# Forming all activation sums of the down projection in the up stage, with its fourth weight combination on VectorE

## The chip, the cores and the metric

The kernel runs on one core of a Trainium2 chip. The metric is the device time of one execution in microseconds (us). Five engines run their own instruction streams in order and wait for each other by semaphores: TensorE (PE in the profile: matrix products; PEld is its weight load), VectorE (DVE), ScalarE (ACT), GpSimd (POOL) and SyncE (SP), which here only issues DMAs. All times below come from the profile of one execution, or from the three timed runs where that is said.

## The reference

One inference step of a decoder layer in float32, for 512 prompt tokens and 64 sample tokens (8 sequences of 8), 576 columns together:

```python
h = rms_norm(x, norm1)
proj = h @ w_in                       # short conv, dilated attention, pooling
x = x + jnp.concatenate([ya, yb, yc], axis=-1) @ w_out
h2 = rms_norm(x, norm2)
gc, new_ffn = causal_dwconv(h2 @ w_gate, ffn_buf, ffn_conv_w)
x = x + (jax.nn.silu(gc) * (h2 @ w_up)) @ w_down
```

The model width is 2048 and the inner width D_FF is 5504, which is 43 tiles of 128. The outputs are the normed rows and the updated caches and states. This case is about the last line: the activations (43 tiles of 128 x 576) are made in the up stage, written to DRAM, and multiplied by `w_down` in the down stage.

## The kernel before

Every float32 operand is split into a high part in fp32r (a copy on ScalarE) and a low part (what is left, a subtraction on VectorE). A product is then three matmuls: high by high, high by low, low by high.

From the gate projection on, products are made in the Strassen-Winograd form (`strassen_steps`). A pair of 128-column output tiles and the two halves of the inner dimension make a 2x2 matrix of weights, b11, b12, b21, b22; the two 288-column halves of the tokens make the other side. Seven products replace eight. Their weights are, in the order of the steps:

- p1: b11
- s1 (p5 in the code's names of places): b12 - b11
- s2 (u2): b22 - (b12 - b11)
- p2: b21
- s3 (u3): b22 - b12
- s4 (p53): b22
- c21: b21 minus the s2 weights, the fourth combination. Before, GpSimd forms it (L1009) in b21's own tile.

In a step the combination is formed (L990, L998, L1005 on VectorE), the result is split (L933 on ScalarE, L934 on VectorE), the product runs on TensorE (L945), and its sum is taken out of the accumulator. In the down stage that is one addition on VectorE (L1487) for each of six products; a copy on ScalarE (L985) starts the second accumulator. The split weights wh and wl have three buffers each, so a split waits until the product three places earlier is done.

The raw weights lie in tiles of two kinds, wr and wx, with three buffers each, and `raw_tile` alternates between them: b11 and b22 fall into wr, b12 and b21 into wx. SyncE issues the loads in program order, and a load waits on that queue until the last reader of its buffer is done. With three wr buffers, the b22 of a pair takes the buffer of the b11 of the pair before.

The gate and up projections (43 column tiles, 168 matmuls in a pair of tiles) fill the up stage, to about 2060 us. The down stage runs in four chunks of ten activation tiles (NDC = 4, DCHUNK = 5); a chunk is eight pairs of output tiles, a pair has 7 x 15 = 105 matmuls. Three activation tiles are left for a last part.

On the token side each step needs its own combination. For each index i of a chunk (an even tile ae and an odd tile ao) there are four "pieces": "11" (half of ae), "s12", "own" (ao) and "s34". For chunk 0, `first_pieces` reads the sums s12 and s34 from DRAM; `sums` has made them in the up stage for the first five pairs (`if ff < 2 * DCHUNK`). For chunks 1 to 3, `act_pieces` loads ae and ao during the chunk before, forms the sums on VectorE (L1445, L1446, L1452) and splits the pieces (L1442 and L1443, L1455 and L1456, L1453). `PIECE_DUE` says after which step of the chunk each piece is written into the program; what is left over is laid between the first five steps of the next chunk (`going`), where the first two pairs are interleaved. The `late` pair (m == 2) loads its b22 only in its third step.

The order on each engine is made by a scheduler that simulates the program; `high_priority` moves the splits of the first two pairs of each chunk forward.

Of the kernel before, what the change touches and what calls it, by code (L numbers as in the profile page):

```python
# [10 lines left out]
F32 = mybir.dt.float32  # L11
F32R = mybir.dt.float32r
AF = mybir.ActivationFunctionType
# [23 lines left out]
DCHUNK = 5  # L37
NDC = 4
X_TILES = (2, 2, 2, 2, 4, 4)
PIECE_DUE = (4, 8, 12, 16, 19, 22, 25, 28, 31, 34, 37, 40, 46, 47, 47, 48, 49, 50, 51)  # L40
LAST_DUE = (4, 10, 14, 18)
FIRST_PIECES = (2, 3, 2, 2, 2, 2)
AHEAD = (7, 11)
# [40 lines left out]
def decoder_step(ctx: ExitStack, tc, I, O):  # L84
# [883 lines left out]
    def strassen_steps(load, X, evac, split, n, urgent=False, late=False):  # L968


        w = n * P
        strn[0] += 1
        tag = "s" if strn[0] % 2 else "pt"
        c = X.c

        def first():
            return tc.high_priority(offset=200) if urgent else nullcontext()

        a, b = bank("a")[:, :HALF], bank("b")[:, :HALF]
# [12 lines left out]
        product(e, hl, c["s1"], True)  # L992
        evac("p5", e)
        yield
        b22 = load(1, 1) if late else b22
        b21 = load(1, 0)
        with first():
            nc.vector.tensor_sub(b11[:, :w], b22[:, :w], b11[:, :w])  # L998
            hl = split(w, b11[:, :w])
        product(a, hl, c["s2"], False)  # L1000
        evac("u2", a)
        yield
        with first():
            hl = split(w, b21[:, :w])
            nc.vector.tensor_sub(b12[:, :w], b22[:, :w], b12[:, :w])  # L1005
        product(b, hl, c["12"], False)
        evac("p2", b)
        yield
        nc.gpsimd.tensor_sub(b21[:, :w], b21[:, :w], b11[:, :w])  # L1009
        with first():  # L1010
            hl = split(w, b12[:, :w])
        product(a, hl, c["s3"], False)
        evac("u3", a)
        yield
        with first():
            hl = split(w, b22[:, :w])
        product(e, hl, c["s4"], False)
        evac("p53", e)
        yield
        with first():  # L1020
            hl = split(w, b21[:, :w])
        product(a, hl, c["22"], False)
        evac("c21", a)
        yield
# [214 lines left out]
    def state_out(nst, f0, nf):  # L1239
# [4 lines left out]
        for f in range(nf):  # L1244
# [14 lines left out]

    def sums(i, g1, g2):  # L1260
# [21 lines left out]
        now.setdefault(kind, []).append(name)  # L1282
        return slot_of(name)

    def first_pieces(X, n):

        half = [work() for _ in range((n + 1) // 2)]
        for i in range(n):
            j = i % 2 * HALF
            dma(half[i // 2][:, j:j + HALF], act_d[2 * i][:, :HALF])  # L1290

        def load(src):
            t = work()
            dma(t, src)
            return t

        raw = {("s12", i): load(sum_d[i][0]) for i in range(n)}
        yield
        for i in range(n):
            if i % 2 == 0:  # L1300
                t11 = next_slot("11")
            hl = single_of(t11, i % 2)
            src = half[i // 2][:, i % 2 * HALF:(i % 2 + 1) * HALF]
            with_unit(nc.scalar.activation(hl[0], src, AF.Copy))
            nc.vector.tensor_sub(hl[1], src, hl[0].bitcast(F32))
            X.put("11", i, hl)
            yield
        todo = [(c, i) for c in ("s12", "own", "s34") for i in range(n)]
        for c, i in todo:
            if c == "own" and i == 0:  # L1310
                raw.update({("own", k): load(act_d[2 * k + 1]) for k in range(n - 1)})
            if c == "own" and i == n - 1:
                raw.update({("own", n - 1): load(act_d[2 * n - 1])})
                raw.update({("s34", k): load(sum_d[k][1]) for k in range(n)})
            t = next_slot(c)
            src = raw[c, i]
            with_unit(nc.scalar.activation(t[:, 0], src, AF.Copy))
            nc.vector.tensor_sub(t[:, 1], src, t[:, 0].bitcast(F32))
            for name, hl in zip({"s12": ("s2", "s1"), "own": ("12", "22"), "s34": ("s4", "s3")}[c], pair_of(t)):
                X.put(name, i, hl)  # L1320
            yield

    x1 = []
# [16 lines left out]
    for nf in GROUPS:  # L1340
# [8 lines left out]
        if f0 == 0:  # L1349
            begun = {0: gate_pair(ht, 0, 0, urgent=True), 2: gate_pair(ht, 2, 2, urgent=True, late=True)}  # L1350
            advance(begun[0][2], 3)
            advance(begun[2][2], 2)
        for f in range(0, nf, 2):
            ff = f0 + f
            if f + 1 < nf:
# [20 lines left out]
            if ups and nf > 1:  # L1376
                for _ in up_steps(*ups.pop(0)):
                    pass
                go_on(len(later))
# [4 lines left out]


    nextX = Halves(DCHUNK)
    nxt = first_pieces(nextX, DCHUNK)
    steps = up_steps(*ups.pop(0))
    next(steps)
    next(nxt)  # L1390
    free.extend(n_ for k in RELEASE for n_ in rest[k])
    for n_ in FIRST_PIECES:
        next(steps)
        for _ in range(n_):
# [18 lines left out]

    AL = 6

    def act_tile(k):
        t = fp.tile([P, TOK], F32, tag="al", bufs=AL, name=nm("al"))
        dma_paced(t, act_d[k])
        return t

    def act_pieces(X, k0, n):

        al, t11 = [], {}
        order_ = [(c, i) for i in range(n - 2) for c in ("11", "s12", "own", "s34")]
        order_ += [(c, i) for i in (n - 2, n - 1) for c in ("11", "s12")]
        order_ += [(c, i) for c in ("own", "s34") for i in (n - 2, n - 1)]
        names = {(c, i): free.pop(0) for c, i in order_ if c != "11" or i % 2 == 0}
        for (c, _), name in names.items():
            now.setdefault(c, []).append(name)

        def load():
            if len(al) < n:
                i = len(al)
                al.append((act_tile(k0 + 2 * i), act_tile(k0 + 2 * i + 1)))

        def piece(c, i):
            ae, ao = al[i]
            if c == "11":
                if i % 2 == 0:
                    t11[i // 2] = slot_of(names[c, i])  # L1440
                hl = single_of(t11[i // 2], i % 2)
                with_unit(nc.scalar.activation(hl[0], ae[:, :HALF], AF.Copy))  # L1442
                nc.vector.tensor_sub(hl[1], ae[:, :HALF], hl[0].bitcast(F32))  # L1443
                X.put("11", i, hl)
                nc.vector.tensor_add(ae[:, HALF:], ae[:, HALF:], ao[:, HALF:])  # L1445
                nc.vector.tensor_sub(ae[:, :HALF], ae[:, HALF:], ae[:, :HALF])  # L1446
                return
            t = slot_of(names[c, i])
            src = ae if c == "s12" else ao
            if c == "s34":  # L1450
                s2 = ae[:, :HALF].unsqueeze(1).to_broadcast([P, 2, HALF])
                with_unit(nc.vector.tensor_sub(halves(ao), halves(ao), s2))  # L1452
                nc.scalar.activation(t[:, 0], src, AF.Copy)  # L1453
            else:
                with_unit(nc.scalar.activation(t[:, 0], src, AF.Copy))  # L1455
            nc.vector.tensor_sub(t[:, 1], src, t[:, 0].bitcast(F32))  # L1456
            for name, hl in zip({"s12": ("s2", "s1"), "own": ("12", "22"), "s34": ("s4", "s3")}[c], pair_of(t)):
                X.put(name, i, hl)
            if c == "s34":
                load()  # L1460

        for _ in range(AL // 2):
            load()
        yield
        for c, i in order_:
            piece(c, i)
            yield

    def last_pieces(k0, n):

# [23 lines left out]
    for ci in range(NDC):  # L1494
# [2 lines left out]
            chunk_done()  # L1497
        if ci < NDC - 1:
            nextX = Halves(DCHUNK)
            nxt = act_pieces(nextX, f0 + nf, DCHUNK)  # L1500
            due = PIECE_DUE
        else:
            nxt = last_pieces(f0 + nf, NF - f0 - nf)
# [17 lines left out]
            pass  # L1521
        if ci == 0:
            chunk_done()
        for steps in pairs:
            load_x1(min(KD, len(x1) + 2))
            for _ in steps:
# [126 lines left out]
```

## Time and profile before

| | |
|---|---|
| three timed runs, median (lowest, highest) | 2643.67 us (2643.23, 2647.12) |
| the profiled execution, its own time | 2641.39 us |
| its span, first to last instruction | 2639.5 us |
| mean granted TensorE clock | 0.988 |
| busy: PE, DVE, ACT, POOL | 2551.3, 1920.6, 972.1, 622.8 us |

The busy time of PE is no measure of its pace, since matmuls overlap. In a stretch the count of matmuls says more: where nothing is waited for, the stretch from 2480 to 2562 us shows 619 of them in 82 us, 7.55 for each us.

### The profile page before, as it was taken

What the parts mean: (1) busy time and instruction counts of PE and PEld (TensorE: products, weight loads), DVE (VectorE), ACT (ScalarE), POOL (GpSimd) and SP (SyncE); (2) the same over time, 40 slices, a digit from 0 to 9 for tenths busy, and PEclk for the clock granted to TensorE, in tenths of its full rate; (3) what the DMA queues carried; (4) which work ended last, traced back from release to release, by engine and by line L of the source; (5) the groups of instructions that cost most, each with busy time, mean ns of one, the idle gap of its engine ahead of it and who ended that gap; (6) DMA issues with size and microseconds to landing.
All of it is one profiled execution on the core that took longest, in us unless ns stands there. A gap on an engine that the chain in (4) does not pass through costs nothing.

```text
span 2639.5 us, 48741 instructions
## 1 busy us (share of the span) xinstructions
PE 2551.3 (97%) x19855; PEld 2495.6 (95%) x19855; DVE 1920.6 (73%) x2619; ACT 972.1 (37%) x1445; POOL 622.8 (24%) x460
## 2 busy tenths in 40 slices
PE   8999989989999999999999999999999999989997
PEld 7999889989989999999999999999999998989897
DVE  5667766865766544597878787877777888888875
ACT  6121221222121233354444444444444544444445
POOL 0434334434443000022222121212121111101014
PEclk9999989989999999999999999999999999999999
DMA  8547457537655696556555555555555865555534
GB/s 272 140 122 182 134 148 194 164 110 197 167 152 168 179 281 196 162 181 194 172 185 157 177 153 169 161 166 161 169 162 175 286 183 152 148 147 168 160 100 150
DMA packets 608210, 451.47 MB, mean 171 GB/s; under 512 B 22967, under 2 KB 570082, under 8 KB 601586
## 3 DMA queue, kind: packets, MB, share of 16 engines
q1 hardware_dynamic: 591358, 438.72, 56.0%
q10 hardware_dynamic: 16628, 9.64, 1.2%
q8 instruction: 156, 2.56, 0.4%
q14 instruction: 68, 0.56, 0.1%
HBM read 402.75 MB, written 132.81 MB: 203 GB/s over the span
## 4 chain that ended last, share of the span: by engine, by line
PE 83%; DVE 8%; DMA 6%; issue 1%; ACT 1%; SPq 0%; POOL 0%; DVEq 0%; ACTq 0%
PE a L945 27%; PE acc L176 11%; PE acc L178 10%; PE acc L177 10%; PE pt L945 7%; PE s L945 6%; PE b L945 6%; DMA ev<-in_cache_kv_w_dram 2%; DVE wl L934 2%; DMA al<-act 1%; DVE av L594 1%; DVE xs L1456 1%; DMA wr<-in_w_down_dram 1%; DVE wl L153 1%; PE ps L569 1%
## 5 line engine op out<-in xcount | busy, mean ns | idle before, releaser
L945 PE MATMUL a<-xs,wh 128*128 128x288 f32 x4032 | 814.4, 296 | 14.2 <-ACT wh L933 8.4
L945 PEld LDWEIGHTS a<-xs,wh 128*128 128x128 f32 x4032 | 647.7, 189 | 21.0 <-ACT wh L933 10.7
L176 PE MATMUL acc<-xs,wh 128*128 128x288 f32 x2208 | 663.4, 301 | 0.0
L177 PE MATMUL acc<-xs,wh 128*128 128x288 f32 x2208 | 657.1, 298 | 0.4 <-DVE xs L203 0.3
L178 PE MATMUL acc<-xs,wl 128*128 128x288 f32 x2208 | 655.9, 297 | 0.2 <-DVE wl L153 0.2
L945 PE MATMUL a<-xs,wl 128*128 128x288 f32 x2016 | 592.6, 295 | 1.6 <-DVE wl L934 1.6
L933 ACT ACTIVATE wh<-wr 128x1024 fp32r<-128x1024 f32 (+1 forms) x300 | 276.7, 924 | 519.7 <-PE a L945 210.9
L176 PEld LDWEIGHTS acc<-xs,wh 128*128 128x128 f32 x2208 | 417.5, 189 | 8.4 <-issue 7.6
L178 PEld LDWEIGHTS acc<-xs,wl 128*128 128x128 f32 x2208 | 419.5, 190 | 4.4 <-issue 3.9
L177 PEld LDWEIGHTS acc<-xs,wh 128*128 128x128 f32 x2208 | 418.5, 190 | 1.7 <-DVE xs L200 0.6
L945 PEld LDWEIGHTS a<-xs,wl 128*128 128x128 f32 x2016 | 378.5, 188 | 2.9 <-DVE wl L934 2.7
L1009 POOL TENSOR_TENSOR wx<-wx,wr 128x1024 f32<-128x1024 f32 (+1 forms) x75 | 161.7, 2157 | 883.3 <-DVE wl L934 747.7
L152 ACT ACTIVATE wh<-wr 128x1024 fp32r<-128x1024 f32 (+1 forms) x150 | 155.4, 1037 | 581.7 <-PE acc L177 505.3
L934 DVE TENSOR_TENSOR wl<-wr,wh 128x1024 fp32r<-128x1024 f32 (+1 forms) x300 | 316.1, 1055 | 73.1 <-ACT wh L933 70.0
L934 DVE TENSOR_TENSOR wl<-wx,wh 128x1024 fp32r<-128x1024 f32 (+1 forms) x225 | 273.8, 1223 | 84.7 <-ACT wh L933 84.5
L153 DVE TENSOR_TENSOR wl<-wr,wh 128x1024 fp32r<-128x1024 f32 (+1 forms) x150 | 242.7, 1619 | 105.5 <-ACT wh L152 99.1
L933 ACT ACTIVATE wh<-wx 128x1024 fp32r<-128x1024 f32 (+1 forms) x225 | 206.5, 921 | 169.7 <-PE b L945 85.9
L945 PE MATMUL s<-xs,wh 128*128 128x288 f32 x1024 | 208.0, 295 | 0.0
L945 PE MATMUL b<-xs,wh 128*128 128x288 f32 x1008 | 206.7, 296 | 0.3
L945 PE MATMUL pt<-xs,wh 128*128 128x288 f32 x992 | 203.1, 297 | 3.7 <-ACT wh L933 3.7
L499 POOL TENSOR_TENSOR eq<-qb,ek 128x1024 f32<-128x1024 f32 x48 | 123.1, 2565 | 224.7 <-DMA ek<-in_cache_kv_w_dram 104.4
L499 POOL TENSOR_TENSOR prod<-qb,ek 128x1024 f32<-128x1024 f32 x48 | 122.7, 2557 | 189.6 <-PE acc L176 102.6
(321 smaller groups left out, 3662.5 us busy)
## 6 DMA issues: line engine op xcount, KB each, us to landing
out_dram<-in_cache_kv_w_dram SPq DMA_DIRECT2D x320, 204.0 KB
wr<-in_w_in_dram SPq DMA_DIRECT2D x110, 512.0 KB
ek<-in_cache_kv_w_dram SPq DMA_DIRECT2D x52, 512.0 KB
ev<-in_cache_kv_w_dram SPq DMA_DIRECT2D x52, 512.0 KB
wx<-in_w_gate_dram SPq DMA_DIRECT2D x43, 512.0 KB
wr<-in_w_gate_dram SPq DMA_DIRECT2D x43, 512.0 KB
wr<-in_w_up_dram SPq DMA_DIRECT2D x43, 512.0 KB
wx<-in_w_up_dram SPq DMA_DIRECT2D x43, 512.0 KB
```

The costliest lines, as they stand in the source:

```text
L152: nc.scalar.activation(hi[:, :n], dst, AF.Copy)
L153: low.tensor_sub(lo[:, :n], dst, hi[:, :n].bitcast(F32))
L176: mark.append(nc.tensor.matmul(o, wh, xh, start=first, stop=False))
L177: nc.tensor.matmul(o, wh, xl, start=False, stop=False)
L178: nc.tensor.matmul(o, wl, xh, start=False, stop=last)
L499: with_unit(nc.gpsimd.tensor_mul(pv_, c["q"], keys))
L569: nc.tensor.matmul(o[32 * j:32 * j + 32, :P], pm[:, c:c + 32], rhs, start=i < 4, stop=i >= len(terms) - 4, tile_position=(0, 32 * j), skip ...
L594: i_ = nc.vector.scalar_tensor_tensor(av[:, t, :], v[:, t, :], w, av[:, t, :], op0=ALU.mult, op1=ALU.add)
L933: nc.scalar.activation(hi[:, :n], src, AF.Copy)
L934: nc.vector.tensor_sub(lo[:, :n], src, hi[:, :n].bitcast(F32))
L945: mm = nc.tensor.matmul(o, a[:, ws], b, start=first and k == 0 and i == 0, stop=k == n - 1 and i == 2, skip_group_check=True)
L1009: nc.gpsimd.tensor_sub(b21[:, :w], b21[:, :w], b11[:, :w])
```

## The change

All sums of the down stage's activations, for 20 pairs of tiles and not for 5, are now made in the up stage and stored in DRAM (`sum_d` has NDC * DCHUNK entries). One `act_pieces` serves all four chunks: it loads the needed piece itself (half tiles for "11", s12, ao, s34) and only splits it. The pieces come in the order "11", "s12", "own", "s34" for the whole chunk, with six (chunk 0: eight) loads ahead, and at other steps than before. The fourth weight combination is written into b11's tile instead of b21's, one step earlier, and in the down projection (n = 5) it is made by VectorE; in the gate and up projections (n = 8) it stays on GpSimd. The late pair gets a step of its own for the load of its b22. In the up stage the extra `go_on` after each pair is left out.

```diff
-PIECE_DUE = (4, 8, 12, 16, 19, 22, 25, 28, 31, 34, 37, 40, 46, 47, 47, 48, 49, 50, 51)
+PIECE_DUE = (2, 5, 8, 11, 14, 17, 20, 23, 27, 31, 35, 39, 42, 45, 46, 48, 50)
...
-        b22 = load(1, 1) if late else b22
+        if late:
+            b22 = load(1, 1)
+            yield
         b21 = load(1, 0)
...
             nc.vector.tensor_sub(b12[:, :w], b22[:, :w], b12[:, :w])
+            (nc.gpsimd if n == 8 else nc.vector).tensor_sub(b11[:, :w], b21[:, :w], b11[:, :w])
         product(b, hl, c["12"], False)
         evac("p2", b)
         yield
-        nc.gpsimd.tensor_sub(b21[:, :w], b21[:, :w], b11[:, :w])
...
         with first():
-            hl = split(w, b21[:, :w])
+            hl = split(w, b11[:, :w])
         product(a, hl, c["22"], False)
...
-             for i in range(DCHUNK)]
+             for i in range(NDC * DCHUNK)]
...
-        if ff < 2 * DCHUNK:
+        if ff < 2 * NDC * DCHUNK:
             sums(ff // 2, g1, g2)
...
+    def act_pieces(X, c, tile_, dma_, ahead_):
...
+        todo = [(kind, i) for kind in ("11", "s12", "own", "s34") for i in range(n)]
...
+        def load(kind, i):
+            t = raw[kind, i] = tile_()
+            r = n * c + i
+            dma_(t, {"s12": sum_d[r][0], "own": act_d[k0 + 2 * i + 1], "s34": sum_d[r][1]}[kind])
...
+            with_unit(nc.scalar.activation(d0, src, AF.Copy))
+            nc.vector.tensor_sub(d1, src, d0.bitcast(F32))
...
-                nc.vector.tensor_add(ae[:, HALF:], ae[:, HALF:], ao[:, HALF:])
-                nc.vector.tensor_sub(ae[:, :HALF], ae[:, HALF:], ae[:, :HALF])
...
-                with_unit(nc.vector.tensor_sub(halves(ao), halves(ao), s2))
```

The new order on VectorE in the middle of a chunk (chunk 2). wl<-wr, wl<-wx are low parts of weights, L1487 takes a product out, L1456 splits a piece. Before, from the split of b22 of one pair to the s2 combination of the next:

```order
L934 TENSOR_TENSOR wl_26031<-wr_25918,wh_26030 128x640
L1487 TENSOR_TENSOR wk_22956<-b_25913,wk_22956 128x288
L934 TENSOR_TENSOR wl_26051<-wx_25962,wh_26050 128x640
L1487 TENSOR_TENSOR wk_22958<-a_25912,wk_22958 128x288
L934 TENSOR_TENSOR wl_26085<-wr_26078,wh_26084 128x640
L990 TENSOR_TENSOR wr_26078<-wx_26080,wr_26078 128x640
L1487 TENSOR_TENSOR wk_22958<-pt_25940,wk_22958 128x288
L1456 TENSOR_TENSOR xs_26070<-al_25783,xs_26070 128x576
L1005 TENSOR_TENSOR wx_26080<-wr_26082,wx_26080 128x640
L934 TENSOR_TENSOR wl_26107<-wr_26078,wh_26106 128x640
L1487 TENSOR_TENSOR wk_22956<-a_25912,wk_22956 128x288
L998 TENSOR_TENSOR wr_26078<-wr_26082,wr_26078 128x640
```

The same stretch now (L1467 takes a product out, L1341 splits a piece, L1007 and L1000 are the former L1005 and L998):

```order
L934 TENSOR_TENSOR wl_25154<-wr_25034,wh_25153 128x640
L1467 TENSOR_TENSOR wk_23316<-b_25029,wk_23316 128x288
L934 TENSOR_TENSOR wl_25174<-wr_25030,wh_25173 128x640
L1341 TENSOR_TENSOR xs_25148<-al_24554,xs_25148 128x576
L1467 TENSOR_TENSOR wk_23318<-a_25028,wk_23318 128x288
L934 TENSOR_TENSOR wl_25205<-wr_25198,wh_25204 128x640
L990 TENSOR_TENSOR wr_25198<-wx_25200,wr_25198 128x640
L1467 TENSOR_TENSOR wk_23318<-pt_25061,wk_23318 128x288
L1007 TENSOR_TENSOR wx_25200<-wr_25202,wx_25200 128x640
L934 TENSOR_TENSOR wl_25227<-wr_25198,wh_25226 128x640
L1467 TENSOR_TENSOR wk_23316<-a_25028,wk_23316 128x288
L1000 TENSOR_TENSOR wr_25198<-wr_25202,wr_25198 128x640
```

The third row, the split for c21, now reads b11's tile (wr) and no longer b21's (wx); the first reader of the next b22 (L1007) stands six rows behind it.

On SP in the middle of chunk 0 (wr and wx are the weights, the copies between them are cache rows from DRAM to DRAM). Before, the loads of one pair, b11, b12, b21 and, fifth, b22:

```order
L1511 DMA wr_24029<-in_w_down_dram 128x5x128 [waits DMAHW1_49,DVE_49]
L1511 DMA wx_24031<-in_w_down_dram 128x5x128 [waits DMAHW2_49,DVE_49]
L1511 DMA wx_24081<-in_w_down_dram 128x5x128 [waits DMAHW3_49,DVE_49]
L140 DMA out_dram<-in_cache_kv_w_dram 16x3264 [waits DMAHW4_49]
L1511 DMA wr_24033<-in_w_down_dram 128x5x128 [waits DMAHW5_49,Pool_49]
L140 DMA out_dram<-in_cache_kv_w_dram 16x3264 [waits DMAHW6_49]
```

Now, b21 (wx_24052) and b22 (wr_24008) of one pair, then b12 and b11 of the next, then a piece:

```order
L1491 DMA wx_24052<-in_w_down_dram 128x5x128 [waits DMAHW7_49,DVE_49]
L140 DMA out_dram<-in_cache_kv_w_dram 16x3264 [waits DMAHW0_49]
L140 DMA out_dram<-in_cache_kv_w_dram 16x3264 [waits DMAHW1_49]
L140 DMA out_dram<-in_cache_kv_w_dram 16x3264 [waits DMAHW2_49]
L1491 DMA wr_24008<-in_w_down_dram 128x5x128 [waits DMAHW3_49,DVE_49]
L1491 DMA wx_24174<-in_w_down_dram 128x5x128 [waits DMAHW4_49]
L1491 DMA wr_24172<-in_w_down_dram 128x5x128 [waits DMAHW5_49,DVE_49]
L140 DMA al_23977<-s34e_11944 128x576 [waits DMAHW6_49,DVE_49]
```

The load of b22 waited for POOL (the reader of b11 was L1009) and stood one copy behind b21; it now waits for DVE (the reader is the c21 split of the pair before) and stands three copies behind b21.

On VectorE at the start of chunk 1, where pair 0 ends and pair 1 (the late one) goes on. Before:

```order
L934 TENSOR_TENSOR wl_24383<-wr_24217,wh_24382 128x640
L1487 TENSOR_TENSOR wk_22786<-b_24212,wk_22786 128x288
L934 TENSOR_TENSOR wl_24403<-wx_24269,wh_24402 128x640
L998 TENSOR_TENSOR wr_24294<-wr_24437,wr_24294 128x640
L1005 TENSOR_TENSOR wx_24296<-wr_24437,wx_24296 128x640
```

Now:

```order
L934 TENSOR_TENSOR wl_24523<-wr_24351,wh_24522 128x640
L1467 TENSOR_TENSOR wk_22933<-b_24346,wk_22933 128x288
L934 TENSOR_TENSOR wl_24557<-wr_24347,wh_24556 128x640
L1467 TENSOR_TENSOR wk_22935<-a_24345,wk_22935 128x288
L1000 TENSOR_TENSOR wr_24429<-wr_24500,wr_24429 128x640
L1007 TENSOR_TENSOR wx_24431<-wr_24500,wx_24431 128x640
```

In both, pair 1's b22 (wr_24437, wr_24500) is first read two or so rows behind pair 0's c21 split; now that split is also the last reader of the buffer (b11 of pair 0, wr_24347) into which this b22 is loaded.

## Rows read from the trace of the kernel before

**Rows 1.** Windows: length, busy (instructions) of PE, PEld, DVE, ACT, POOL; clock, DMA, GB/s
```profile
1188.00:2046.00 858.00, 858.00 (x6478) 857.77 (x6478) 671.79 (x821) 372.99 (x475) 192.32 (x189) 1.00 0.55 169
2080.00:2106.00 26.00, 22.76 (x153) 20.38 (x152) 23.47 (x37) 12.02 (x20) 2.04 (x1) 1.00 1.06 363
2106.00:2204.00 98.00, 94.96 (x698) 92.61 (x697) 86.39 (x132) 43.79 (x69) 13.86 (x7) 1.00 0.58 169
2204.00:2233.00 29.00, 23.41 (x150) 22.70 (x149) 21.35 (x34) 9.80 (x15) 3.12 (x2) 0.88 0.48 151
2233.00:2328.00 95.00, 92.00 (x678) 89.78 (x677) 83.41 (x127) 43.18 (x68) 11.71 (x6) 1.00 0.53 154
2328.00:2359.00 31.00, 25.21 (x162) 23.92 (x161) 23.68 (x37) 10.01 (x16) 3.12 (x2) 0.89 0.54 162
2359.00:2455.00 96.00, 93.21 (x688) 91.21 (x687) 84.63 (x129) 43.55 (x69) 11.71 (x6) 1.00 0.51 149
2455.00:2480.00 25.00, 20.33 (x143) 18.81 (x142) 20.39 (x31) 9.72 (x15) 1.57 (x1) 1.00 0.60 200
2480.00:2562.00 82.00, 82.00 (x619) 81.80 (x618) 67.36 (x99) 32.31 (x48) 9.44 (x6) 1.00 0.42 123
```

**Rows 2.** Waits of PE from 2204 to 2233 us: total, times, longest
```profile
PE pt L945 <- DVE wl L934: 2.4, 1, 2.4
PE a L945 <- ACT wh L933: 2.1, 1, 2.1
```

**Rows 3.** Groups by line and shape, 2040 to 2580 us: busy us, mean ns
```profile
L934 DVE TENSOR_TENSOR wl<-wr,wh 128x640 fp32r<-128x640 f32 x128 | 105.7, 828 | 20.1 <-ACT wh L933 19.3
...
L934 DVE TENSOR_TENSOR wl<-wx,wh 128x640 fp32r<-128x640 f32 x96 | 84.8, 898 | 6.4 <-ACT wh L933 6.4
...
L1009 POOL TENSOR_TENSOR wx<-wx,wr 128x640 f32<-128x640 f32 x32 | 58.1, 1817 | 441.2 <-DVE wl L934 391.9 <-DMA act<-wk 27.2 <-PE s L945 12.3
...
L1456 DVE TENSOR_TENSOR xs<-al,xs 128x576 fp32r<-128x576 f32 x45 | 49.7, 1108 | 0.0
...
L1452 DVE TENSOR_TENSOR al<-al,al 128x576 f32<-128x576 f32 x15 | 11.2, 749 | 1.7 <-PE s L945 1.7
...
L1445 DVE TENSOR_TENSOR al<-al,al 128x288 f32<-128x288 f32 x15 | 8.2, 544 | 7.9 <-DMA al<-act 7.9
...
L1446 DVE TENSOR_TENSOR al<-al 128x288 f32<-128x288 f32 x15 | 6.5, 446 | 0.0
```

**Rows 4.** Timeline of POOL and DVE near 2180 us: start, duration, instruction
```profile
2180.20 2.03 POOL L1009 TENSOR_TENSOR wx<-wx,wr 128x640 f32<-128x640 f32 x1 [12.01 <-DVE wl L934]
...
2180.72 2.13 DVE L1456 TENSOR_TENSOR xs<-al,xs 128x576 fp32r<-128x576 f32 x1
```

**Rows 5.** Timeline of DVE and PE in the last chunk, 2541 to 2552 us
```profile
2541.91 0.83 DVE L934 TENSOR_TENSOR wl<-wx,wh 128x640 fp32r<-128x640 f32 x1 [0.24 <-ACT wh L933]
...
2545.80 0.81 DVE L1005 TENSOR_TENSOR wx<-wr,wx 128x640 f32<-128x640 f32 x1
...
2549.34 0.82 DVE L934 TENSOR_TENSOR wl<-wr,wh 128x640 fp32r<-128x640 f32 x1 [0.89 <-ACT wh L933]
...
2551.19 0.29 PE L945 MATMUL a<-xs,wl 128*128 128x288 f32 x1
```

**Rows 6.** Timelines of SP and DVE, 2212 to 2227 us: DMA issues, their readers
```profile
2212.77 0.32 SPq L140 DMA_DIRECT2D al<-act  x1
...
2215.72 0.46 DVE L1445 TENSOR_TENSOR al<-al,al 128x288 f32<-128x288 f32 x1 [0.42 <-DMA al<-act]
...
2220.98 0.48 SPq L1511 DMA_DIRECT2D wr<-in_w_down_dram  x1
...
2222.57 0.83 DVE L934 TENSOR_TENSOR wl<-wx,wh 128x640 fp32r<-128x640 f32 x1 [0.24 <-ACT wh L933]
...
2226.17 0.83 DVE L998 TENSOR_TENSOR wr<-wr,wr 128x640 f32<-128x640 f32 x1 [2.77 <-DMA wr<-in_w_down_dram]
```

**Rows 7.** Groups on DVE, 1188 to 1386 us: the last of the three sums
```profile
L1271 DVE TENSOR_TENSOR wk<-wk,wk 128x576 f32<-128x576 f32 x5 | 3.8, 758 | 0.2
```

More of the change, by code (lines that the diff above doesn't have):

```diff
@@ L1283, in next_slot @@
         return slot_of(name)
[L1285 to L1297, printed above, removed]
-        yield
[L1299 to L1320, printed above, removed]
@@ new lines, in act_pieces, with load11, load_to @@
+    def act_pieces(X, c, tile_, dma_, ahead_):
+        n = DCHUNK
+        k0 = 2 * n * c
+        todo = [(kind, i) for kind in ("11", "s12", "own", "s34") for i in range(n)]
+        names = {}
+        loads = []
+        raw = {}
+        def load11(i):
+            t = tile_()
+            for k in range(i, min(i + 2, n)):
+                part = t[:, (k - i) * HALF:(k - i + 1) * HALF]
+                dma_(part, act_d[k0 + 2 * k][:, :HALF])
+                raw["11", k] = part
+        def load(kind, i):
+            t = raw[kind, i] = tile_()
+            r = n * c + i
+            dma_(t, {"s12": sum_d[r][0], "own": act_d[k0 + 2 * i + 1], "s34": sum_d[r][1]}[kind])
+        for kind, i in todo:
+            if kind != "11":
+                loads.append((kind, i))
+            elif i % 2 == 0:
+                loads.append((kind, i))
+        at_ = 0
+        def load_to(m):
+            nonlocal at_
+            while at_ < min(m, len(loads)):
+                kind, i = loads[at_]
+                load11(i) if kind == "11" else load(kind, i)
+                at_ += 1
+        load_to(ahead_)
+        yield
+        for kind, i in todo:
+            if kind != "11" or i % 2 == 0:
+                names[kind, i] = free.pop(0)
+                now.setdefault(kind, []).append(names[kind, i])
+        for j, (kind, i) in enumerate(todo):
+            src = raw[kind, i]
+            if kind == "11":
+                if i % 2 == 0:
+                    t11 = slot_of(names[kind, i])
+                d0, d1 = single_of(t11, i % 2)
+                X.put("11", i, (d0, d1))
+            else:
+                t = slot_of(names[kind, i])
+                d0, d1 = t[:, 0], t[:, 1]
+                for name, hl in zip({"s12": ("s2", "s1"), "own": ("12", "22"), "s34": ("s4", "s3")}[kind], pair_of(t)):
+                    X.put(name, i, hl)
+            with_unit(nc.scalar.activation(d0, src, AF.Copy))
+            nc.vector.tensor_sub(d1, src, d0.bitcast(F32))
+            del raw[kind, i]
+            done_ = loads.index((kind, i - i % 2 if kind == "11" else i)) + (kind != "11" or i % 2 or i + 1 == n)
+            load_to(done_ + ahead_)
@@ L1352, in decoder_step @@
             advance(begun[2][2], 2)
+            advance(begun[0][2], 1)
+            advance(begun[2][2], 1)
         for f in range(0, nf, 2):
@@ L1378, in decoder_step @@
                     pass
-                go_on(len(later))
             if f + 1 < nf:
@@ L1386, in decoder_step @@
     nextX = Halves(DCHUNK)
-    nxt = first_pieces(nextX, DCHUNK)
+    nxt = act_pieces(nextX, 0, work, dma, 8)
     steps = up_steps(*ups.pop(0))
     next(steps)
+    free.extend(n_ for k in RELEASE for n_ in rest[k])
     next(nxt)
-    free.extend(n_ for k in RELEASE for n_ in rest[k])
     for n_ in FIRST_PIECES:
@@ L1414, in decoder_step, with al_tile @@
     AL = 6
+    def al_tile():
+        return fp.tile([P, TOK], F32, tag="al", bufs=AL, name=nm("al"))
     def act_tile(k):
-        t = fp.tile([P, TOK], F32, tag="al", bufs=AL, name=nm("al"))
+        t = al_tile()
         dma_paced(t, act_d[k])
         return t
[L1421 to L1444, printed above, removed]
-                nc.vector.tensor_add(ae[:, HALF:], ae[:, HALF:], ao[:, HALF:])
-                nc.vector.tensor_sub(ae[:, :HALF], ae[:, HALF:], ae[:, :HALF])
[L1447 to L1451, printed above, removed]
-                with_unit(nc.vector.tensor_sub(halves(ao), halves(ao), s2))
[L1453 to L1467, printed above, removed]
     def last_pieces(k0, n):
@@ L1499, in decoder_step @@
             nextX = Halves(DCHUNK)
-            nxt = act_pieces(nextX, f0 + nf, DCHUNK)
+            nxt = act_pieces(nextX, ci + 1, al_tile, dma_paced, AL)
             due = PIECE_DUE
@@ L1523, in decoder_step @@
             chunk_done()
+        next(pairs[0])
+        next(pairs[1])
         for steps in pairs:
```

## Prediction

> **What bounds the kernel now.** I first read the windows [rows 1], because the busy share of PE (97% of the span) hides its pace: matmuls overlap, so I count them. In the stretch from 2480 to 2562 us, 619 matmuls start in 82 us, 7.55 for each us; the up stage from 1188 to 2046 us shows 6478 in 858 us, also 7.55. That is full pace, and a stretch's loss is its length less its matmuls divided by 7.55. The chunk starts lose 26 - 153/7.55 = 5.7 us (chunk 0), 9.1 (chunk 1), 9.5 (chunk 2) and 6.1 (chunk 3), together 30.4. The interiors of chunks 0, 1 and 2 lose 5.5, 5.2 and 4.9, together 15.6; the last chunk's interior loses nothing. So 46.0 us is all that the down stage can give back, and the up stage has nothing to give.
>
> What separates the last interior from the others is VectorE: 86.39/98, 83.41/95 and 84.63/96, all 88% busy, against 67.36/82 = 82% [rows 1]. ScalarE lies at 39 to 45% and DMA between 0.42 and 0.58. The last chunk prepares no pieces for a next one. I read this as VectorE pacing the interiors of chunks 0 to 2.
>
> At a chunk start the waits of PE [rows 2] name the low part of a weight (2.4 us at once) and a high part (2.1 us at once). The second has a transfer behind it: VectorE's combination stood 2.77 us for the late pair's b22 [rows 6]. The granted clock is 0.88 and 0.89 in two of the four starts and 1.00 elsewhere [rows 1], so part of each runs at the lower level, 1.2 GHz and not 2.4, after PE had stood. A share of 0.12 lost over 29 us is 3.5 us, and 0.11 over 31 us is 3.4: 6.9 of the 30.4 us.
>
> **The change part by part.** All sums are against the profiled execution, 2641.39 us by its own time (span 2639.5, 1.9 around it); the median of the three runs is 2.3 us above it, and I take the saving from the median.
>
> *VectorE in the interiors.* The sums of chunks 1 to 3 go: 8.2 + 6.5 + 11.2 = 25.9 us, 8.6 for a chunk [rows 3]. The fourth combination comes: 32 times 0.81 us, the duration of the combination beside it [rows 5], 26 us, 6.5 for a chunk. So far this is an exchange. But GpSimd's 32 instructions (1.817 us each, 58.1 us) go as well, and beside one of them a piece's split on VectorE took 2.13 us [rows 4] against about 0.75 for an operation of the same width, L1452 [rows 3]. The means carry it: 45 splits at 1.108 less 0.749 make 16.2 us, 96 splits from wx at 0.898 less 0.828 make 6.7 us. The pieces' splits lie in three chunks and those from wx in four, so that is 16.2/3 + 6.7/4 = 7.1 us for a chunk. VectorE then has 8.6 + 7.1 - 6.5 = 9.2 us less of some 97 in a chunk, 79% instead of 88%, below the 82% at which nothing is lost. Bounds of the interior's loss by this alone: 0 (last chunk) to 15.6 us (as now).
>
> *Up stage.* Fifteen more pairs of tiles get sums, 0.76 us [rows 7] and two of half the width at 0.45 (L1446, [rows 3]), 1.7 us a pair, 25 us, and two stores each. VectorE there is 671.79/858 = 78% busy, PE at full pace, and in that very window five pairs already have sums. I cost it at nothing. The cover is VectorE's 186 us of idle time; were it gone, the 25 us would show.
>
> *The new wait for b22.* With three wr buffers, b22 of a pair takes b11's of the pair before. Its last reader was GpSimd; it is now the c21 split on VectorE, four products later than b11's own use. In the last chunk [rows 5] that split ends at 2541.91 + 0.83 = 2542.74, and b22's first reader, the combination for s3, starts at 2545.80, 3.1 us after it. It need not start there: the low part for s2 is ready at 2549.34 + 0.82 = 2550.16, and PE's first matmul with it starts at 2551.19, 1.0 us later. A landing up to about 4.0 us after the issue costs PE nothing. Every us beyond costs 1 us in 24 pairs (32 less the two at the head of each chunk). Behind the waiting combination stand the s1 split and the next products' evacuations, which is how it reaches PE; behind the load on SP's queue stand the next pair's b12 and b11 and one piece, which have buffers and time.
>
> Landings, bounded by rows [rows 6]: an activation tile issued at 2212.77 is read at 2215.72 (2.9 us, its reader waiting); a b22 issued at 2220.98, with another load ahead of it, is read at 2226.17 (5.2 us, its reader waiting). In the interiors b22 stands behind three copies of cache rows, which I put between: 3.6 to 4.2 us, at the threshold and nearer to the 2.9 us row, since b21 itself went out long before. I take 5 us for all interiors of chunks 0 to 2 (0.2 us in each of 24 pairs), ends 0 and 24 x 1.2 = 29 us, and 1 us for the last chunk (0 to 6).
>
> [...]
>
> *Chunk starts.* The first gap comes from pieces bunched at steps 46 to 51 and their wait for activation tiles; the pieces are now spread evenly from step 2 on and only split. I take 5.2 us to 2.5 a start. The second gap, the late pair's b22, is now issued only behind pair 0's c21 split, at 2222.57 + 0.83 = 2223.40 instead of 2220.98 [rows 6], 2.4 us later, but with no load just ahead of it; at 2.9 us it lands at 2226.3, as now, at 5.2 us at 2228.6. I keep 2.2 us (0 to 4.7). Half of the low-clock time goes with the first gap. Together 30.4 becomes 22, ends 15 and 36. The start of the up stage has the same dependence once or twice: 2 us (0 to 4).
>
> *Sum.* 46.0 becomes 5 + 1 + 22 + 2 = 30: 16 us saved by the terms, of which I count 14, since the chunk starts are the least certain. 2643.67 - 14 = 2629.5 us. About 5 us (0.2%) is what a measurement of this kernel can tell from no change.
>
> **The rivals.**
> *A: the chunk starts fall too.* If both gaps close, PE does not stand and the clock stays at 1.00 there; the starts fall to 15 or less and the interiors to 2: 28 us, 2615 us. For it: the pieces are spread over the whole chunk. Against: b22 of pair 1 is issued later.
> *B: the wait for b22 takes the gain back.* Landing at 4.6 to 4.9 us costs 0.6 to 0.9 us in 24 pairs, 14 to 22 us: 2638 to 2644 us. For it: the threshold of 4.0 us lies inside the two rows; and the copies ahead of it. Against: DMA is half idle [rows 1].
> *C: slower.* The same mechanism decides from the other end: each b22 lands as when queued behind a load, 5.2 us and a little more for the extra 3.5 instead of 2 tiles loaded for each index. 1.5 us in 24 pairs is 36 us, the starts stay at 30: 2660 to 2665 us. It decides above 4.0 us of landing, and turns to slower at about 4.9.
> *D: an even exchange.* If what stretched VectorE's rows was not GpSimd, 25.9 us out and 26 in leave the interiors at 88%: 2643 us. For it: the longer means of splits could have a cause that stays. Against: 2.13 beside 0.75 us while GpSimd was at work [rows 3, 4].
> The Trainium skill speaks of this ("Perfetto Trace Analysis", section "Optimizing Scalar/DVE Operations"): where VectorE is saturated, work may go from it to GpSimd, though the two share a read port and it might not help. Its first half is against this change, its second for it. By the 2.13 us [rows 4] the second holds here.
>
> **How the numbers follow.** The forecast (2629.5, from 2622 to 2637) 0.52, A 0.15, B 0.17, C 0.11, D 0.05. Faster by over 0.2%, below 2638.4: forecast, A, and a third of B, 0.72. Within 0.2%: D and most of B, 0.17. Slower: C, 0.11. The range from 2614 to 2645 holds the forecast, nearly all of B and D and most of A, and leaves out C.
>
> **What would show it.** Windows of the three interiors at 7.5 matmuls for each us and VectorE near 79% there; no splits of 2 us on VectorE in the down stage; the combination for s3 (now L1007) with an idle time before it that ends by a DMA of under 1 us a pair, and PE without waits behind it; the clock at 1.00 over the chunk starts; the up stage from 1188 us still at 7.55. I am wrong if L1007 or L1000 stand over 1 us for b22 in most pairs (B, C), if the up stage falls behind its pace, or if VectorE stays at 88% (D).

## The result, and the profile after

The changed kernel took 2658.93 us (median of 9 runs, 2652.37 to 2666.45) against 2642.99 us for the kernel before on the same chips: the ratio is 1.0058, 95% interval 1.0043 to 1.0074. It is slower by about 15 us, where 14 us faster was forecast.

I cut both profiled executions at the same products. A chunk's first 210 matmuls (its two interleaved pairs) are its start, the other 630 its interior; the loss is the length less the matmuls divided by 7.55. The windows cut after by these bounds (columns as in [rows 1]) are:

```profile
2087.40:2124.70 37.30, 32.06 (x213) 30.56 (x212) 26.38 (x43) 13.93 (x23) 0.00 (x0) 0.91 0.80 259
2124.70:2219.30 94.60, 88.58 (x632) 84.20 (x632) 75.53 (x119) 40.57 (x64) 0.00 (x0) 1.00 0.63 186
2219.30:2254.20 34.90, 31.08 (x211) 29.53 (x211) 25.64 (x41) 13.23 (x22) 0.00 (x0) 0.95 0.57 178
2254.20:2345.80 91.60, 87.60 (x632) 84.05 (x631) 73.05 (x116) 39.80 (x63) 0.00 (x0) 1.00 0.59 169
2345.80:2381.00 35.20, 31.52 (x213) 29.67 (x212) 25.43 (x40) 13.28 (x22) 0.00 (x0) 0.95 0.58 180
2381.00:2470.90 89.90, 87.74 (x632) 84.00 (x631) 73.50 (x116) 39.77 (x63) 0.00 (x0) 1.00 0.59 170
2470.90:2503.80 32.90, 29.95 (x212) 28.10 (x211) 24.70 (x38) 12.50 (x20) 0.00 (x0) 1.00 0.59 191
2503.80:2592.00 88.20, 85.03 (x628) 83.18 (x627) 65.75 (x103) 33.41 (x51) 1.72 (x2) 1.00 0.37 104
```

At full pace 630 matmuls take 83.4 us. The four interiors (rows two, four, six and eight) take 94.6, 91.6, 89.9 and 88.2. The loss by this cut, in us, each from one profiled execution:

| | up stage | four starts | four interiors | median, us |
|---|---|---|---|---|
| before | 5.8 | 31.3 | 17.7 | 2642.99 |
| changed | 7.8 | 29.1 | 31.5 | 2658.93 |

The two profiled executions differ by 17.6 us of span: 13.8 in the interiors, -2.2 in the starts, 2.0 in the up stage, and 4.2 ahead of the gate projection, where nothing was changed. That last term is scatter: over all kernels of this study the stretch ended between 1113.9 and 1124.2 us, in no order with what was changed. The up stage from 1188 to 2046 us still shows 6479 matmuls in 858 us, its full pace.

What the interiors wait for stands in the groups by line and shape from 2080 to 2590 us (busy us, mean ns, then idle time ahead and its releaser):

```profile
L1341 DVE TENSOR_TENSOR xs<-al,xs 128x576 fp32r<-128x576 f32 x45 | 33.8, 751 | 0.1
...
L1007 DVE TENSOR_TENSOR wx<-wr,wx 128x640 f32<-128x640 f32 x32 | 26.3, 823 | 37.2 <-DMA wr<-in_w_down_dram 37.2
L1000 DVE TENSOR_TENSOR wr<-wr,wr 128x640 f32<-128x640 f32 x32 | 26.1, 817 | 13.9 <-DMA wr<-in_w_down_dram 13.8
L1008 DVE TENSOR_TENSOR wr<-wx,wr 128x640 f32<-128x640 f32 x32 | 26.1, 816 | 0.0
```

L1008 is the new combination: 26.1 us, as worked out. L1341 splits a piece in 0.751 us where L1456 took 1.108 [rows 3]: the stretch beside GpSimd is gone. But L1007, the combination for s3 and the first reader of b22 in most pairs, now stands 37.2 us for its load. In the kernel before, over the same window, the two readers of b22 (L1005 and L998 there) waited for it almost only at the late pairs of the chunk starts (L998):

```profile
L1005 DVE TENSOR_TENSOR wx<-wr,wx 128x640 f32<-128x640 f32 x32 | 26.2, 818 | 0.8 <-DMA wr<-in_w_down_dram 0.7
L998 DVE TENSOR_TENSOR wr<-wr,wr 128x640 f32<-128x640 f32 x32 | 26.2, 818 | 9.8 <-DMA wr<-in_w_down_dram 9.7
```

One wait of L1007, in the timeline of the changed kernel in chunk 0 (start, duration, instruction, idle time ahead in brackets):

```profile
2149.87 1.79 SPq L140 DMA_DIRECT2D out_dram<-in_cache_kv_w_dram  x3
...
2150.44 0.82 DVE L934 TENSOR_TENSOR wl<-wr,wh 128x640 fp32r<-128x640 f32 x1
...
2151.75 0.53 SPq L1491 DMA_DIRECT2D wr<-in_w_down_dram  x1
...
2152.16 0.83 DVE L934 TENSOR_TENSOR wl<-wr,wh 128x640 fp32r<-128x640 f32 x1 [0.18 <-ACT wh L933]
...
2159.37 0.82 DVE L1007 TENSOR_TENSOR wx<-wr,wx 128x640 f32<-128x640 f32 x1 [2.91 <-DMA wr<-in_w_down_dram]
2160.11 0.82 DVE L934 TENSOR_TENSOR wl<-wr,wh 128x640 fp32r<-128x640 f32 x1
...
2160.99 0.40 PE L945 MATMUL pt<-xs,wl 128*128 128x288 f32 x1 [1.30 <-DVE wl L934]
```

Read from the top: three copies are issued, then b22 at 2151.75. L1007 starts at 2159.37, 7.6 us later, as soon as it has landed. Behind L1007 stands the split for s1 (2160.11), and TensorE waits for that split (2160.99), though s1 needs nothing of b22.

The rows also correct the prediction, and the section on the change, on who releases the buffer. b22 is issued behind the split of 2150.44, which is that of the preceding pair's b22 (for s4), and ahead of the end of the c21 split (2152.16 + 0.83 = 2152.99). In the program's placement of tiles a b22 takes the preceding pair's b11 before the change, and in the changed kernel the preceding pair's b22, in every pair: b11's tile now lives up to the c21 split, so b22's own is the first to come free. In the last listing of that section the releasing split is the first row (wl_24523 from wr_24351) and not the third.

Over the 32 pairs, counted from the issue to the last of a load's 16 landing events, b22 lands after 6.03 us (median); in the kernel before it was 4.89.

### The profile page after: what moved, and what is told of

It reads as the page before. It is cut to its first block, busy times and chain, and to the rows that moved or that the text cites. A ratio compares the mean times of both kernels' runs of the same rounds, so it can differ in the third digit from the quotient of the medians.

```text
span 2657.1 us, 48811 instructions
## 1 busy us (share of the span) xinstructions
PE 2564.5 (97%) x19855; PEld 2501.1 (94%) x19855; DVE 1958.9 (74%) x2651; ACT 966.4 (36%) x1445; POOL 598.7 (23%) x428
## 5 line engine op out<-in xcount | busy, mean ns | idle before, releaser
L933 ACT ACTIVATE wh<-wr 128x1024 fp32r<-128x1024 f32 (+1 forms) x375 | 345.9, 923 | 623.8 <-PE a L945 211.5
L934 DVE TENSOR_TENSOR wl<-wr,wh 128x1024 fp32r<-128x1024 f32 (+1 forms) x375 | 394.0, 1051 | 76.7 <-ACT wh L933 74.9
L152 ACT ACTIVATE wh<-wr 128x1024 fp32r<-128x1024 f32 (+1 forms) x150 | 155.4, 1037 | 586.8 <-PE acc L177 528.7
L153 DVE TENSOR_TENSOR wl<-wr,wh 128x1024 fp32r<-128x1024 f32 (+1 forms) x150 | 245.2, 1636 | 103.9 <-ACT wh L152 99.8
L1008 POOL TENSOR_TENSOR wr<-wx,wr 128x1024 f32<-128x1024 f32 x43 | 139.8, 3250 | 648.2 <-DVE wl L934 570.8
L934 DVE TENSOR_TENSOR wl<-wx,wh 128x1024 fp32r<-128x1024 f32 (+1 forms) x150 | 184.3, 1236 | 16.7 <-ACT wh L933 16.0
L945 PEld LDWEIGHTS s<-xs,wh 128*128 128x128 f32 x1024 | 164.0, 188 | 5.9 <-ACT wh L933 4.3
L945 PEld LDWEIGHTS b<-xs,wh 128*128 128x128 f32 x1008 | 163.0, 189 | 5.7 <-ACT wh L933 5.4
```

Source lines behind the costliest of these rows:

```text
L152: nc.scalar.activation(hi[:, :n], dst, AF.Copy)
L153: low.tensor_sub(lo[:, :n], dst, hi[:, :n].bitcast(F32))
L933: nc.scalar.activation(hi[:, :n], src, AF.Copy)
L934: nc.vector.tensor_sub(lo[:, :n], src, hi[:, :n].bitcast(F32))
L945: mm = nc.tensor.matmul(o, a[:, ws], b, start=first and k == 0 and i == 0, stop=k == n - 1 and i == 2, skip_group_check=True)
L1008: (nc.gpsimd if n == 8 else nc.vector).tensor_sub(b11[:, :w], b21[:, :w], b11[:, :w])
```

## The experiments

Each kernel is the changed one with one edit, where nothing else is said. The reference of each ratio is the kernel before on the same chip.

**The tile of the combination.** VectorE forms it still, in b21's tile, one step later.

```diff
-            (nc.gpsimd if n == 8 else nc.vector).tensor_sub(b11[:, :w], b21[:, :w], b11[:, :w])
+            if n == 8:
+                nc.gpsimd.tensor_sub(b11[:, :w], b21[:, :w], b11[:, :w])
...
         evac("p2", b)
         yield
+        if n != 8:
+            with first():
+                nc.vector.tensor_sub(b21[:, :w], b21[:, :w], b11[:, :w])
```

> The changed kernel, but in the down stage VectorE writes the fourth combination into b21's tile, one step later, so that b11's buffer is free after that combination and not after the c21 split. Theory 1 (the wait for b22): b22 is issued two products earlier, its landing of 6.0 us (median of the changed kernel) ends before its reader, the loss of the interiors falls from 31.5 us to 10 or less, and the time to 2630 to 2640 us. Theory 2 (the work itself, 26 us more on VectorE and more bytes loaded): nothing of that is changed, the time stays at 2655 to 2663 us.

Measured: 2618.77 us, ratio 0.9915 (0.9891 to 0.9938). Interiors 4.1 us, starts 18.0. The same 32 instructions on the same engine, written into another tile, make 38 us less (0.9915 against 1.0058). The interior of chunk 1:

```profile
2240.90:2325.20 84.30, 83.95 (x631) 83.45 (x631) 72.48 (x116) 39.77 (x63) 0.00 (x0) 1.00 0.63 189
```

VectorE is busy for 72.48 us here and for 73.05 in the changed kernel: the work is the same, the wait is gone.

**The sums alone**, with the combination on GpSimd in b21's tile as before:

```diff
-            (nc.gpsimd if n == 8 else nc.vector).tensor_sub(b11[:, :w], b21[:, :w], b11[:, :w])
...
         yield
+        nc.gpsimd.tensor_sub(b21[:, :w], b21[:, :w], b11[:, :w])
```

> The changed kernel with the fourth combination as it was before (GpSimd, b21's tile): only the sums have moved. Theory 1: b22 is released as before, VectorE has 25.9 us less in chunks 0 to 2; interiors at 10 us or less, 2630 to 2640 us. Theory 2, in the form that the extra loads (3.5 tiles for each index instead of 2) are the price: 2655 us or more.

Measured: 2620.48 us, 0.9922 (0.9897 to 0.9946); interiors 9.4, starts 18.3. Moving the sums, with the new order of the pieces that comes with it, is the gain, and the 3.5 tiles loaded for each index are not the price. No run separates the sums from the new order.

**The combination alone**, added to the kernel before as the change has it (VectorE, b11's tile):

```diff
             nc.vector.tensor_sub(b12[:, :w], b22[:, :w], b12[:, :w])
+            (nc.gpsimd if n == 8 else nc.vector).tensor_sub(b11[:, :w], b21[:, :w], b11[:, :w])
...
-        nc.gpsimd.tensor_sub(b21[:, :w], b21[:, :w], b11[:, :w])
```

> The kernel before with the fourth combination alone changed (VectorE, b11's tile); sums stay in the down stage. Theory 1: the wait for b22 comes with it and VectorE keeps its sums: interiors lose 30 us or more, the time is 2655 to 2675 us. Theory 2 (the moved loads are the price): 2640 to 2648 us, an even exchange.

Measured: 2662.2 us, 1.008 (1.0062 to 1.0098); interiors 28.5, starts 36.8. The loss is all here, without the moved sums.

**No copies between the weights.** All copies of cache rows are issued ahead of the down stage:

```diff
-    TOTAL_STEPS = 16 * 4 + 43 * 7 + NDC * 8 * 4
+    TOTAL_STEPS = 16 * 4 + 43 * 7
```

> The changed kernel with all copies of cache rows issued in the stages before the down stage, none between its weights. Theory 1: b22 no longer stands behind three copies, its landing falls from 6.0 us towards 4, the interiors' loss from 31.5 us to some 10 us, the time to 2635 to 2642 us if the up stage carries the copies at its pace. Theory 2: interiors as now, 2655 us or more.

Measured: 2624.29 us, 0.9933 (0.9911 to 0.9955). b22 lands after 4.39 us (median), interiors 9.8 us. A b22 of chunk 1, issued with the b11 behind it:

```profile
2260.73 0.82 DVE L934 TENSOR_TENSOR wl<-wr,wh 128x640 fp32r<-128x640 f32 x1
...
2261.57 2.09 SPq L1491 DMA_DIRECT2D wr<-in_w_down_dram  x2
...
2266.66 0.82 DVE L1007 TENSOR_TENSOR wx<-wr,wx 128x640 f32<-128x640 f32 x1
```

It is still released by the s4 split (2260.73 + 0.82), but L1007 starts without a wait. So a landing in about 5 us is early enough, and the copies in the down stage cost the median landing 1.6 us. The up stage, where the copies went, is slower here:

```profile
1188.00:2046.00 858.00, 853.65 (x6430) 851.59 (x6429) 727.55 (x861) 367.46 (x471) 222.41 (x188) 1.00 0.64 197
```

48 matmuls fewer than [rows 1] in the same 858 us are 6.4 us. That the copies are the cause is not shown: by the cut above the whole up stage loses 14.3 us here, but also 13.5 in the next experiment and 10.9 with four buffers, where the edit leaves the up stage as it is in the changed kernel (7.8).

**The engine alone put back**, in b11's tile:

```diff
-            (nc.gpsimd if n == 8 else nc.vector).tensor_sub(b11[:, :w], b21[:, :w], b11[:, :w])
+            nc.gpsimd.tensor_sub(b11[:, :w], b21[:, :w], b11[:, :w])
```

> The changed kernel with the engine alone put back: GpSimd forms the fourth combination in the down stage, but in b11's tile as changed, so that b22 still waits for the c21 split. Theory 1 (the wait for b22, by the choice of the tile): interiors lose 25 us or more, time 2650 to 2668 us. Rival (the 26 us on VectorE): interiors at 10 us, 2620 to 2630 us, as with GpSimd in b21's tile (2620).

Measured: 2654.42 us, 1.004 (1.0025 to 1.0054); interiors 30.0. The tile, not the engine, brings the wait. A piece's split is stretched again:

```profile
L1341 DVE TENSOR_TENSOR xs<-al,xs 128x576 fp32r<-128x576 f32 x45 | 39.5, 877 | 0.2
```

**A fourth wr buffer** in the down stage:

```diff
         if rawn[0] % 2:
+            ring[0] += 1
+            if len(ring) > 1 and ring[0] % 4 == 0:
+                return ring[1].tile([P, DCHUNK * P], F32, tag="wr4", bufs=1, name=nm("wr"))
             return wp.tile([P, 1024], F32, tag="wr", name=nm("wr"))
...
-    AL = 6
+    AL = 5
```

> The changed kernel with a fourth wr buffer in the down stage (and five buffers for activation tiles instead of six, to make room); the combination stays on VectorE in b11's tile. b22 then takes the buffer of the b22 two pairs earlier. Theory 1: b22 is issued before the c21 split and the wait is gone: interiors at 10 us or less, 2615 to 2635 us. Rival (the combination's place itself on VectorE or PE): 2650 us or more.

Measured: 2616.25 us, 0.9895 (0.9872 to 0.9918); interiors 4.0, starts 13.3. The combination stays in b11's tile, and the wait goes with the shortage of buffers. b22 lands no sooner after its issue (median 6.35 us), but it is issued earlier: in the interiors its first reader starts 17.3 us after the issue (median) and never waits for it, where in the changed kernel it starts 6.3 us after the issue and waits in 19 of 24 pairs.

**The combination on VectorE in b21's tile, sums as before** (an edit of the kernel before):

```diff
-        nc.gpsimd.tensor_sub(b21[:, :w], b21[:, :w], b11[:, :w])
+        with first():
+            (nc.gpsimd if n == 8 else nc.vector).tensor_sub(b21[:, :w], b21[:, :w], b11[:, :w])
```

> The kernel before with the fourth combination on VectorE in b21's own tile, and nothing else changed: the sums stay in the down stage. It tells what VectorE's share is worth. If VectorE's total sets the interiors, 6.5 us a chunk come to it and the stretch of 7.1 goes: interiors as before, 16 to 20 us, 2636 to 2645 us. If GpSimd's stretch and not the total was what cost: interiors at 8 us or less, 2625 to 2633 us. If the stretch does not go: interiors at 30 us or more, 2650 us.

Measured: 2626.55 us, 0.9939 (0.9918 to 0.9959); interiors 13.2, starts 20.4. The time lies in the range of the second case, the interiors between the first two: VectorE has 26 us more of its own to do, and the kernel is faster by 16 us.

**b21's tile in both stages**, GpSimd in the up stage, VectorE in the down stage:

```diff
-            (nc.gpsimd if n == 8 else nc.vector).tensor_sub(b11[:, :w], b21[:, :w], b11[:, :w])
...
         yield
+        with first():
+            (nc.gpsimd if n == 8 else nc.vector).tensor_sub(b21[:, :w], b21[:, :w], b11[:, :w])
```

> The changed kernel with the fourth combination in b21's tile in the up stage too (GpSimd there, VectorE in the down stage). Theory 1 says that the up stage's loss, 8.1 us in the changed kernel and 6.1 before, goes back to 6 and all else stays as with b21's tile in the down stage alone: 2614 to 2620 us. Rival: the up stage's loss is the stores of the sums, and stays at 8: 2616 to 2622 us.

Measured: 2614.59 us, 0.9889 (0.9864 to 0.9914). The up stage's loss is 5.6 us, where it was 7.8 (by the cut above; the figures in the expectation are 0.3 us higher), though the stores of the sums are all there. Over all profiles this stage loses 5.4 to 6.7 us with b21's tile there and 7.5 to 14.3 with b11's. So the tile, and not the stores, goes with the 2 us, but single profiles of one and the same up stage differ by more (7.8 to 13.5). Starts 20.0, interiors 4.1.

**Both remedies**, b21's tile and the fourth buffer:

> The combination in b21's tile in both stages (as in the version that took 2614.59 us) and the fourth wr buffer in the down stage as well. If what is left at the chunk starts (20.0 us) is the late pair's b22 waiting for a buffer, the starts fall to 13 us, as with four buffers alone, and the time to 2605 to 2612 us. Rival (b22 is no longer late there, the rest is something else): 2612 to 2618 us.

Measured: 2605.19 us, 0.9856 (0.983 to 0.9881), the fastest kernel here, 38 us below the one before. Starts 12.0, interiors 1.1. Its start and interior of chunk 0, then of chunk 1:

```profile
2079.90:2114.60 34.70, 31.14 (x211) 30.43 (x211) 29.01 (x47) 15.73 (x25) 0.00 (x0) 0.90 0.99 315
2114.60:2198.40 83.80, 83.79 (x633) 83.55 (x632) 72.51 (x117) 39.77 (x63) 0.00 (x0) 1.00 0.69 203
2198.40:2227.90 29.50, 29.09 (x212) 28.01 (x212) 26.07 (x42) 13.36 (x22) 0.00 (x0) 1.00 0.70 207
2227.90:2311.60 83.70, 83.69 (x633) 83.45 (x632) 72.44 (x116) 39.76 (x63) 0.00 (x0) 1.00 0.64 186
```

The start of chunk 0 (34.7 us for 27.8 of work, clock 0.90, DMA busy at 0.99) still loses 7 us, the other starts 1.7 each. In it TensorE waits 2.2 us for a low part and 1.3 for a high part, and a granted clock of 0.90 over 34.7 us costs some 3.5 us more, an estimate.

**The second pair not late**, on top of that:

```diff
-                                        late=m == 2))
+                                        late=False))
```

> The same with the second pair of a chunk no longer late: its b22 is loaded in its first step, since four buffers leave it a place. If the late load is what holds the starts: 10 us or less for the starts, 2600 to 2610 us. Rival: the earlier load waits on SP's queue for its buffer and holds the loads behind it, as late as before or later: 2608 to 2620 us.

Measured: 2612.29 us, 0.9889 (0.9869 to 0.9909): not faster than 2605.19. The starts fall by only 1 us, to 11.0, and the interiors rise to 12.7. The rival was right in its time. Of the 12.7 us, 7.1, 1.5 and 2.2 lie in the first pair of the interiors of chunks 0, 1 and 2. In chunk 0 that pair's b12 is issued 34 us behind the first product of the down stage (22 us in the kernel with both remedies), the s1 combination stands 3.5 us for it on VectorE, and TensorE stands 4.4 us behind that. What put b12 later was not tested.

**The order on VectorE alone.** In the changed kernel L1007 is tied behind L1000, the combination for s2 (the edit stands in the code of all stages):

```diff
-            nc.vector.tensor_sub(b11[:, :w], b22[:, :w], b11[:, :w])
+            u2 = nc.vector.tensor_sub(b11[:, :w], b22[:, :w], b11[:, :w])
...
-            nc.vector.tensor_sub(b12[:, :w], b22[:, :w], b12[:, :w])
+            u3 = nc.vector.tensor_sub(b12[:, :w], b22[:, :w], b12[:, :w])
+            tc.add_manual_dep(u3.ins, u2.ins.name,
+                              mybir.DependencyInfo(mybir.DependencyClass.NoSync, mybir.DependencyReason.DATA),
+                              reason="behind the s2 combination")
```

> The changed kernel with one order on VectorE: the combination for s3 (L1007), b22's first reader, stands behind the combination for s2 (L1000) and so behind the s1 split; b22 is issued as late as in the changed kernel. If the wait reaches TensorE because L1007 holds the s1 split and what follows behind it on VectorE, b22 may land some 2 us later without cost, and with a landing of 6 us the interiors' loss falls from 31.5 us to 8 to 15 us, the time to 2632 to 2645 us. Rival (the s2 combination needs b22 as early as the s1 split needs VectorE): 2652 to 2662 us, with the wait now on the s2 combination.

Measured: 2624.08 us, 0.9941 (0.9917 to 0.9964). b22 takes the same buffer as in the changed kernel and lands after 5.86 us (median), hardly sooner than the 6.03 there, yet the interiors lose 2.6 us. The groups by line (2080 to 2590 us) and the windows of the interiors of chunks 0 and 1:

```profile
L1007 DVE TENSOR_TENSOR wx<-wr,wx 128x640 f32<-128x640 f32 x32 | 26.2, 818 | 0.0
L1000 DVE TENSOR_TENSOR wr<-wr,wr 128x640 f32<-128x640 f32 x32 | 26.2, 818 | 16.7 <-DMA wr<-in_w_down_dram 16.7
```

```profile
2120.90:2206.20 85.30, 84.57 (x631) 83.65 (x632) 75.72 (x119) 40.80 (x64) 0.00 (x0) 1.00 0.70 211
2240.30:2323.70 83.40, 83.40 (x632) 83.40 (x632) 74.40 (x117) 40.26 (x63) 0.00 (x0) 1.00 0.62 185
```

In all, VectorE now stands 16.7 us for b22 and not 37.2 + 13.8 = 51.0, since the s1 split and what follows it are done while b22 is under way. This names how the lateness of b22 reached TensorE in the interiors: through the instruction that waited for it at the head of VectorE's queue. The starts stay at 31.1 in this profile (13.6 of it in chunk 0), where the late pair's b22 still waits for its buffer.

Several expectations above say that b22 waits for the c21 split; by the timeline it is the s4 split one product earlier. The edits test the same thing either way: the tile of the combination, the buffer, what stands ahead of the load, and what stands behind its reader.

## Why the prediction was wrong

The step that failed is the new wait for b22, put at 5 us for the interiors of chunks 0 to 2 and 1 us for the last ("landings ... 3.6 to 4.2 us ... at the threshold"). The interiors' loss went from 17.7 to 31.5 us where it should have fallen to 6. What the runs showed in its place: b22 is released by another instruction than was worked out, lands 6.03 us after its issue, and its first reader, L1007, stands 37.2 us for it in all at the head of VectorE's queue, with the s1 split, which TensorE needs, behind it. Point by point:

- *The wait as a mechanism* was seen, and as rival C even with its size (5.2 us of landing or more, slower, 2660 to 2665 us; 2658.93 measured, just below). It got 0.11.
- *Its releaser* was wrong: the preceding b22's s4 split, not the c21 split. I took the order of the buffers from the kernel before; a longer life of b11's tile changed which buffer comes free first.
- *The landing* was the term most out of size: 6.03 us, not 3.6 to 4.2. I set it between two single rows, 2.9 and 5.2 us [rows 6], and nearer to the load that had nothing ahead of it. The b22 loads of the kernel before, counted one by one, already had a median of 4.89, most of them with one copy ahead; the order showed three now. Without copies it is 4.39. But the landing alone does not decide: with four buffers it is 6.35, and nothing waits, since the issue is earlier.
- *The threshold* of 4.0 us was counted from the c21 split. From the issue that the trace shows, landings of about 4 us cost nothing in the last pairs (4.2 and 4.0 us: loss 0.0), and those of 7.4 and 7.5 us cost 2.6 and 2.2 us a pair.
- *What is queued behind the waiting instruction* was named (the s1 split) but not priced as the way by which the wait decides. Putting L1007 behind L1000 took away 29 of the 31.5 us.
- *VectorE's share as the bound* was a wrong reading. With L1007 behind L1000, the interior of chunk 1 runs at full pace with VectorE busy for 74.40 of 83.40 us, 89%, more than the 88% that I took for the limit [rows 1]. The busy share of the last interior, 82%, was no threshold. What cost the kernel before its 17.7 us goes with the sums in the down stage and with the combination on GpSimd: without the sums 9.4, with the combination on VectorE 13.2, without both (and b22 in time) 4.1. That it is GpSimd's stretch of VectorE's splits, and not another effect of that combination, was not tested by itself.
- *The exchange on VectorE* (26 us in, 25.9 out, the stretch gone) was right: L1008 26.1 us, splits of 0.751 us, no GpSimd instruction in the interiors of chunks 0 to 2. Rival D is refuted.
The Trainium skill ("Perfetto Trace Analysis", section "Optimizing Scalar/DVE Operations") says both that GpSimd may relieve a saturated VectorE and that the port which they share may undo it. The sums left as they were, taking the 32 instructions from GpSimd gave 0.9939 (0.9918 to 0.9959): here its second half holds. With the sums moved the two places are equal within the scatter (0.9915 on VectorE, 0.9922 on GpSimd), and that the port is the reason no run shows.
- *The chunk starts*, 30.4 to 22, would have come: 18.0 and 18.3 us where b22 is released early. In the changed kernel the first gap shrank as forecast (the wait for a low part at the start of chunk 1, 2.4 us in [rows 2], is gone) but the late pair's b22 took it back: in chunk 0 L1000 stood 5.2 us for it. 29.1 is inside my ends of 15 and 36. The term itself was not sound: 5.2 and 2.2 us a start with 6.9 us of low clock make 36.5 and not 30.4, and no row has the 5.2.
- *The up stage* at no cost for the sums, 2 us for its start: 7.8 against 5.8, and 5.6 with b21's tile.
- *The sum* is 2643.67 - 14 = 2629.67, not 2629.5; nothing hangs on it.

So the moved sums, with the new order of the pieces, are worth 20 us (2620.48 against 2640.78), the combination on VectorE in b21's tile 16 us alone and within the scatter on top of the sums (2618.77 against 2620.48); the tile chosen for it costs 1.0058 against 0.9915, some 38 us.

What stays open: what makes the splits late at the start of chunk 0 even in the fastest kernel, what puts b12 later where the second pair is not late, why the start of chunk 0 loses 13.6 us with L1007 behind L1000, and what the loss in the up stage beyond its start comes from.

## What to carry to other kernels

When an edit lets an instruction write into another tile, look at whose life gets longer and which buffer the next load gets then; with few buffers the pool hands out another one than before. Price a load's landing from the same load in the same place, all of them, with what stands ahead of it on its queue, not from the best row. And where an instruction may wait, look at what is behind it on its engine: putting one instruction behind another was worth some 31 us here (1.0058 to 0.9941 of the kernel before), with the load about as late as ever.

## What the runs showed of the hardware that was not expected

The b22 load of 327,680 bytes landed after 4.39 us where no copy stood between the down stage's weights on SP's queue, after 4.98 us in the kernel before where one copy stood just ahead of it, and after 6.18 us in the changed kernel where three did (medians; most copies are of 204 KB). The copies just ahead are not all of it: in the changed kernel's 12 pairs with none just ahead the median was 5.76 us, and one load took 7.37. VectorE at 89% busy let TensorE run at full pace, the 630 matmuls of an interior in 83.4 us. A VectorE split of 128 x 576 took 0.751 us on average with GpSimd idle, and 0.877, 0.928 and 1.108 us in three kernels where GpSimd formed the combination (in b11's tile, in b21's with the sums moved, and before).
